# Convolution taps held at their written place on VectorE, and the layer norm's sums taken with the convolutions

## The chip, the cores and the metric

The kernel runs on one core of one Trainium2 chip. That core has five engines with instruction queues of their own: TensorE (PE, matrix multiplication; the loading of its stationary operand is shown apart as PEld), VectorE (DVE), ScalarE (ACT), GpSimd (POOL) and SyncE (SP), which here only issues DMA transfers. They meet through semaphores. The metric is the device time of one execution in microseconds (us); less is better.

## What is computed

One layer of a streaming encoder: 512 rows (time steps) of width 2048, float32. Cut to what matters here, where `h` is the normalised input, and `proj = h @ w_in` is split into its parts:

```python
qkv, z_a, b_raw, a_raw, glu_in, z_b, gate_logits = jnp.split(proj, _split_points(), axis=-1)
...
o_a = gated_delta_chunked(q, k, v, g_log, beta)      # 16 heads; inverts a 64x64 triangle per chunk
o_a = rmsnorm(o_a, g_dn_out[i]).reshape(B, S, DN_WIDTH).astype(x.dtype) * jax.nn.silu(z_a)
y_a = o_a @ w_br_a[i]
u = jax.nn.glu(glu_in, axis=-1)
u = causal_depthwise_conv(u, w_dw[i]) + b_dw[i]      # 31 taps along time, for each channel
u = jax.nn.silu(layernorm(u, ln_g[i], ln_b[i])) * jax.nn.silu(z_b)
y_b = u @ w_br_b[i]
...
mixed = (gate_a * y_a + gate_b * y_b) @ w_out[i]
x = x + rmsnorm(mixed, g_post[i])
e = p[i] @ w_ple_proj[i]
x = x + rmsnorm(jax.nn.sigmoid(x @ w_ple_gate[i]) * e, g_ple[i])
```

The layer norm goes over the 2048 channels of each time step; in the kernel channels lie on partitions, 128 to a tile, so that its sums run over 16 tiles and then over the partitions.

## The kernel before

**Matmuls.** A float32 operand is split into a high and a low part; each product is three matmuls of 128x512 (high·high, high·low, low·high). `gemm_cm` makes one 128x512 output tile from 16 pieces along the depth, so 48 matmuls in one PSUM bank (L181, L183, L185). Its weights come by SP as `raw` tiles of 512 KB. ScalarE casts the high part (L127), VectorE subtracts for the low one (L128), and up to three such pieces are prepared ahead.

**Jobs, ticks and side work.** The tiles of `gemm_cm` are queued as `jobs`. After every matmul `tick()` counts down each generator in `active`; one whose count is used up runs to its next `yield n`, which sets the next count (its own period if no n is given). So all other work is *written* between the matmuls of the gemms at a chosen number of ticks. The framework then works out each engine's order from what was written, and may place an instruction earlier or later among those of its engine; `pin(...)` (`keep_in_program_order`) holds one at its written place. Before the change only the multiplications of the inverse (L900) are pinned.

**Stages, in order.**

1. Load and transpose the input; form the operands of the block products.
2. `z_phase`: z and the gated pair (GLU) by seven block products (P1, Q5, P6, P7, P3, P2, Q4) in six blocks `jp`: before the change the first two are z, the other four the gated pair. A gated block's result is transposed and stored as `u0_dram`, the input of the convolutions.
3. 64 tiles of `gemm_cm`, and one for beta: q, k, v of the 16 heads, with silu(z_b) and gate tiles between. After every six q/k/v tiles a generator `group(g)` for two heads is spawned: transposes; `pg` (L866, the products of keys and queries); W; copies into `Ud` on ScalarE (L882); the transpose UT (L889) on VectorE; the triangular inverse, 31 pairs of multiplication and sum on VectorE (L900, L901); its transposes Vd (L908) and Tc (L916); after 22 ticks `py` on TensorE (L922), the first to read Tc; `pz` (L925) and `pd` (L937); then two scans over the chunks (`head_scan`), whose psA, psB and psS on TensorE alternate with short work on VectorE (`Xz`, S) and ScalarE. There are eight groups.
4. Branch A: `o_a` is split (`split_oa`), 16 tiles multiply it by `w_br_a`. Sums for the later `w_out` products run on GpSimd's DMA queue (`presum`).
5. The layer norm, while left-over gate tiles run; then branch B (`w_br_b`), which needs all 16 normalised tiles and begins with `finish()`, so with all side work done.
6. The output products, the embedding gate, and the output.

**The convolutions** run beside stages 2 to 4, tile by tile of 128 channels. `dwconv(i)` loads a tile `u`, starts `uc` on ScalarE (L307), adds 30 taps on VectorE (L310), loads the next tile at tap 22, adds the result to `acc`, and stores it. One `yield` per tap makes a step. Steps come from `conv_side` in stage 2 (every second call, from block 3 on), then by a pace: `tempo[0]` ticks to a step, 14 in stage 3 and 4.9 in branch A. `group` sets the pace to 0 at its start, grants 11 steps behind the Ud copies (`H_BURST`), and turns the pace on again at Vd. `convs()` ends when all tiles are done.

The layer norm before: reload 16 tiles, mean by one matmul with ones (L1066), subtract it, square, add the squares, variance by four one-column matmuls (L1081), then scale, silu, multiply with z_b and split.

`slots` is a pool of 21 SBUF tiles of 128x512; `s2` and `lop` take over the memory of the heads in stage 4.

Of the kernel before, what the change touches and what calls it, by code (L numbers as in the profile page):

```python
# [15 lines left out]
P = 128  # L16
T = 512
# [65 lines left out]
def _body(ctx, tc, A, out):  # L83
# [203 lines left out]


    u_t = [None] * NK
    done = [0]  # L290
    acc = []
    cpool = [slots, "s"]

    u_in = {}

    def load_u(i):
        u_in[i] = cpool[0].tile([P, T], F32, tag=cpool[1], name="u")
        nc.sync.dma_start(u_in[i], u0_dram[i])

    def dwconv(i):  # L300
        w0 = V_DW + i * TAPS
        if i == 0:
            load_u(0)
            yield
        u = u_in.pop(i)
        y = cpool[0].tile([P, T], F32, tag=cpool[1], name="uc")
        nc.scalar.activation(y, u, AF.Identity, scale=vv(w0 + TAPS - 1), bias=vv(V_BDW + i))  # L307
        yield
        for s in range(1, TAPS):
            nc.vector.scalar_tensor_tensor(y[:, s:], u[:, 0:T - s], vv(w0 + TAPS - 1 - s), y[:, s:], ALU.mult, ALU.add)  # L310
# [11 lines left out]
    tempo = [0, 0]  # L322

    def convs():
        n = 0
        for i in range(NK):
            for _ in dwconv(i):
                n += 1
                yield int(tempo[0] * n) - int(tempo[0] * (n - 1)) if tempo[0] else 3
                while not tempo[0] and not tempo[1]:  # L330
                    yield 2
                if not tempo[0]:
                    tempo[1] -= 1
    conv = convs()


# [17 lines left out]
    def z_phase():  # L354
# [166 lines left out]
        def conv_side():  # L521
            side2[0] += 1
            if side2[0] % 2:
                tempo[:] = [9, 0]
                next(conv)

        for jp in range(6):
            glu = jp >= 2
            conv_on = conv_side if jp >= 3 else None
            more = stepper(gen, 2)  # L530
            ps = run(("P1", "Q5"), (lambda: (more(), conv_side())) if jp >= 4 else more)
            for _ in gen:
# [13 lines left out]
            for t in range(2):  # L546
                tt_(d[t], ps["P3"][t], d[t], ALU.add)
                tt_(s5[t], s5[t], u2[t], ALU.subtract)
                for n, c in ((0, d[t]), (2, s5[t])):
                    if glu:  # L550
                        nc.scalar.activation(c, c, AF.Sigmoid)
                    else:
                        fin(n + t, 2 * jp + 1, c)
            ps = run(("P2", "Q4"), conv_on)
            for t in range(2):
                tt_(s1[t], ps["P2"][t], s1[t], ALU.add)
                tt_(u2[t], ps["Q4"][t], u2[t], ALU.add)
                for n, c, g in ((0, s1[t], d[t]), (2, u2[t], s5[t])):
                    if glu:
                        tt_(c, c, g, ALU.mult)  # L560
                    else:
                        fin(n + t, 2 * jp, c)
            gen = transposed(4 * (jp - 2), (s1, u2)) if glu else iter(())
        finish("form")
# [3 lines left out]
    FILL = 5  # L568
    H_TEMPO, H_BURST = 14, 11
    z_phase()  # L570
    tempo[:] = [H_TEMPO, 0]
    spawn(conv, H_TEMPO, "conv")
    gemm_cm(w_in_tile(BA_TILE), hT, lambda ps: spawn(beta_decay(ps), 5))
# [132 lines left out]

    o_a = [None] * NH

    def conv4(ps, ct):
# [33 lines left out]
    def head_scan(g, hh, G):  # L743
# [62 lines left out]
        for x in range(2):  # L806
            nc.vector.tensor_scalar(oav[:, :, x, :], po[:, :, 1 - x, :], vv(V_GDN), None, ALU.mult)
        o_a[h] = oa

    def group(g):  # L810
        tempo[:] = [0, 0]
        G = dict(ke=[], vh=[])
# [37 lines left out]
        for hh, h, s4, kq, kc, vc in heads:  # L850
# [30 lines left out]
        for r, n, b in ((slice(0, P), P, 0), (slice(32, 64), 32, 32), (slice(96, P), 32, 32)):  # L881
            nc.scalar.copy(Ud[r], U[r, :, b:b + 32].rearrange("p x s -> p s x").unsqueeze(2).broadcast_to([n, 32, 4, 8]))  # L882
        tempo[1] = H_BURST
        yield
        VT = hd.tile([P, 32, 8], F32, tag="VT", name="VT", bufs=1)
# [25 lines left out]
        for qd in (0, 2, 1, 3):  # L911
# [4 lines left out]
            nc.vector.transpose(Tc[r, :, b:b + 32], dst)  # L916
        yield 22
        pz = wps.tile([P, 8, 64], F32, tag="w", name="pz")
# [66 lines left out]
    oT = []  # L985

    def split_oa():
        for h in range(NH):
            oh = low(2 * h, "oh")
            nc.scalar.copy(oh, o_a[h])  # L990
# [47 lines left out]

    jobs.append(lambda: tempo.__setitem__(0, 4.9))
    for _ in range(3):  # L1040
# [5 lines left out]
    for i in range(NK):  # L1046
        gemm_cm(A["w_br_a"][i], oT, evac_ya(i))
        if i + 3 < NK:
            jobs.append(lambda i=i: load_gate(i + 3))
        if i < 7:  # L1050
            rest.popleft()()
# [6 lines left out]
    def layer_norm():  # L1058
        while done[0] < NK:
            yield  # L1060
        for i in range(NK):
            u_t[i] = s2.tile([P, T], F32, tag="s2", name="ur")
            nc.sync.dma_start(u_t[i], u_dram[i])
            yield 3
        pm = lps.tile([P, T], F32, tag="l", name="mean_ps")
        mm(pm, ones, acc[0], start=True, stop=True)  # L1066
        mean = low(0, "mean", F32)
        nc.vector.tensor_scalar(mean, pm, 1.0 / D, None, ALU.mult)
        acc2 = low(0, "acc2", F32)
        for i in range(NK):  # L1070
# [7 lines left out]
        yield  # L1078
        pvr = lps.tile([P, T], F32, tag="l", name="var_ps")
        for tt in range(NTT):  # L1080
            mm(pvr[:, tt:tt + 1], acc2[:, tt * P:(tt + 1) * P], ones[:, 0:1], start=True, stop=True)  # L1081
        yield
        var = lnp.tile([P, NTT], F32, name="var")
        nc.vector.tensor_scalar(var, pvr[:, 0:NTT], 1.0 / D, EPS, ALU.mult, ALU.add)
        rst = lnp.tile([P, NTT], F32, name="rst")
# [13 lines left out]
        for i in range(NK):  # L1099
            u = u_t[i]  # L1100
            nc.vector.tensor_tensor(u, u, rstd, ALU.mult)
            nc.scalar.activation(u, u, AF.Silu, scale=vv(V_LNG + i), bias=vv(V_LNB + i))
# [9 lines left out]
            yield  # L1112

    def load_zb(i):
        zb[i] = low(0, "zb", F32)
        nc.sync.dma_start(zb[i], zb_dram[i])

    jobs.append(lambda: spawn(layer_norm(), 7))
    while rest:
# [485 lines left out]
```

## Time and profile before

| | |
|---|---|
| median of 3 runs | 2524.67 us (2522.82 to 2525.76) |
| profiled execution | 2530.41 us, of which the span from first to last instruction is 2528.6 us |
| TensorE busy | 2469.2 us |
| VectorE busy | 1852.9 us |
| ScalarE busy | 1162.8 us |
| GpSimd busy | 218.0 us |
| mean granted TensorE clock | 0.981 |
| convolution taps (L310) | 480 in all, 342.2 us |
| DMA | 386.51 MB, 153 GB/s |

How to read it: busy time is the union of an engine's instructions. Matmuls are pipelined, so that one of 0.39 us may begin 0.23 us after the one before; a busy TensorE is not one at its peak. The profile gives for each instruction group its line, engine, tiles and shapes, busy time, mean duration in ns, and the idle time of the engine ahead of it with what ended it. The view of waits has us in total, times, and the longest. A row of the windows view has the stretch, its length, and the busy time and number of instructions of each engine (or of one line alone), then the granted clock as a share of the full one, the DMA engines' share and GB/s. A row of the timeline has start, duration, engine, line, operation, output and inputs, and in brackets the idle time before it and what ended that.

### The profile page before, as it was taken

The page shows a single profiled execution, that of the slowest core. Times are in us where ns is not written, and L with a number is a line of the kernel's source. Part 1 is how long each engine was busy: PE and PEld are TensorE (multiplying, and loading weights), DVE is VectorE, ACT ScalarE, POOL GpSimd, SP SyncE. Part 2 cuts the span into 40 slices and gives each one's busy share as a digit, 9 for nine tenths or more (in the row PEclk, how much of TensorE's full clock was granted, in tenths as well). Part 3 has the DMA queues.
Part 4 walks back from the last instruction along what each step waited for, and adds up shares of the span by engine and source line. Part 5 has one row for each costly group of instructions (what it writes and reads, how often), then busy time and mean ns, then how long its engine had stood idle before and what let it go on. Part 6 is the DMA issues. An engine that isn't in the chain of part 4 may idle for free.

```text
span 2528.6 us, 33524 instructions
## 1 busy us (share of the span) xinstructions
PE 2469.2 (98%) x11978; PEld 2013.1 (80%) x11978; DVE 1852.9 (73%) x3539; ACT 1162.8 (46%) x2287; POOL 218.0 (9%) x292
## 2 busy tenths in 40 slices
PE   8999999999999999999999999999999999999998
PEld 7888878878878787878878788888788888788886
DVE  7878779788677777777786869899736655567644
ACT  6545544455635454445546364522225623444532
POOL 0000000011000000000100000232312100000000
PEclk9999999999989898989999899999999999999999
DMA  7576655554322222323222223798957733564642
GB/s 262 168 197 184 183 169 165 176 159 134 115 78 88 72 100 72 100 69 111 78 94 82 94 71 109 221 274 258 297 184 214 263 120 105 201 228 166 206 173 75
DMA packets 147592, 386.51 MB, mean 153 GB/s; under 512 B 16608, under 2 KB 29152, under 8 KB 147424
## 3 DMA queue, kind: packets, MB, share of 16 engines
q1 hardware_dynamic: 125920, 327.73, 38.6%
q0 software_dynamic: 20352, 54.54, 9.6%
q10 hardware_dynamic: 1152, 2.10, 0.3%
q8 instruction: 94, 1.54, 0.2%
q14 instruction: 74, 0.61, 0.1%
HBM read 331.87 MB, written 52.43 MB: 152 GB/s over the span
## 4 chain that ended last, share of the span: by engine, by line
PE 72%; DVE 18%; issue 4%; ACT 3%; DMA 2%; SPq 0%; POOL 0%; DVEq 0%; POOLq 0%; ACTq 0%
PE g L185 12%; PE g L181 12%; PE g L183 12%; DVE uc L310 7%; PE zp L479 5%; PE zp L481 5%; PE zp L480 5%; DVE w L128 3%; DVE prod L900 2%; PE f L1292 2%; PE f L1293 2%; PE f L1291 2%; PE f L1457 2%; PE f L1455 2%; PE f L1456 2%
## 5 line engine op out<-in xcount | busy, mean ns | idle before, releaser
L185 PE MATMUL g<-hh,w 128*128 128x512 f32 x1552 | 624.2, 402 | 5.8 <-DVE w L128 5.8
L183 PE MATMUL g<-hl,w 128*128 128x512 f32 x1552 | 624.4, 402 | 0.0
L181 PE MATMUL g<-hh,w 128*128 128x512 f32 x1552 | 622.4, 401 | 0.0
L127 ACT CAST w<-raw 128x512 fp32r<-128x512 f32 x588 | 358.4, 618 | 514.4 <-PE g L185 383.1
L128 DVE TENSOR_TENSOR w<-raw,w 128x512 fp32r<-128x512 f32 x588 | 405.3, 693 | 227.1 <-ACT w L127 225.2
L185 PEld LDWEIGHTS g<-hh,w 128*128 128x128 f32 x1552 | 296.4, 191 | 65.6 <-DVE w L128 9.8
L310 DVE SCALAR_TENSOR_TENSOR uc<-u,vec,uc 128x503 f32<-128x503 f32 (+22 forms) x480 | 342.2, 732 | 3.1 <-ACT uc L307 0.9
L183 PEld LDWEIGHTS g<-hl,w 128*128 128x128 f32 x1552 | 296.0, 191 | 57.6 <-issue 2.1
L181 PEld LDWEIGHTS g<-hh,w 128*128 128x128 f32 x1552 | 296.2, 191 | 56.5 <-issue 1.1
L714 DVE SCALAR_TENSOR_TENSOR cv<-g,vec,cv 128x511 f32<-128x511 f32 x144 | 107.0, 743 | 26.0 <-ACT cv L712 25.4
L479 PE MATMUL zp<-w,zoh 128*128 128x512 f32 x256 | 101.6, 397 | 0.0
L181 PE MATMUL g<-oh,w 128*128 128x512 f32 x256 | 99.8, 390 | 1.5 <-ACT w L127 1.5
L481 PE MATMUL zp<-w,zol 128*128 128x512 f32 x256 | 100.7, 393 | 0.0
L185 PE MATMUL g<-oh,w 128*128 128x512 f32 x256 | 100.1, 391 | 0.6 <-DVE w L128 0.6
L480 PE MATMUL zp<-w,zoh 128*128 128x512 f32 x256 | 99.8, 390 | 0.8 <-DVE w L361 0.8
L183 PE MATMUL g<-ol,w 128*128 128x512 f32 x256 | 99.6, 389 | 0.0
L181 PE MATMUL g<-uh,w 128*128 128x512 f32 x256 | 99.6, 389 | 0.0
L183 PE MATMUL g<-ul,w 128*128 128x512 f32 x256 | 99.6, 389 | 0.0
L185 PE MATMUL g<-uh,w 128*128 128x512 f32 x256 | 99.6, 389 | 0.0
L466 ACT CAST w<-zt 128x512 fp32r<-128x512 f32 x96 | 59.4, 621 | 71.6 <-PE zp L481 50.1
L900 DVE TENSOR_TENSOR prod<-UT,VT 128x2 f32<-128x2 f32 (+30 forms) x248 | 87.9, 354 | 3.2
L1014 POOL DMA_DIRECT2D wsum<-in_w_out x96 | 75.2, 819 | 137.1 <-DMA g_dram<-gt 46.5
(372 smaller groups left out, 4565.0 us busy)
## 6 DMA issues: line engine op xcount, KB each, us to landing
raw<-in_w_in SPq DMA_DIRECT2D x194, 512.0 KB, 3.3
raw<-in_w_glu SPq DMA_DIRECT2D x48, 512.0 KB, 4.1
wsum<-in_w_out POOLq DMA_DIRECT2D x96, 256.0 KB, 6.4
raw<-in_w_ple_gate SPq DMA_DIRECT2D x40, 512.0 KB, 3.4
zraw<-in_w_glu SPq DMA_DIRECT2D x64, 256.0 KB, 4.7
raw<-in_w_br_a SPq DMA_DIRECT2D x32, 512.0 KB, 6.3
wo_sums<-wsum POOLq DMA_DIRECT2D x64, 256.0 KB, 5.4
raw<-in_w_br_b SPq DMA_DIRECT2D x32, 512.0 KB, 3.3
```

Of the source, the lines that this page charges most:

```text
L127: nc.scalar.copy(hi, rq)
L128: nc.vector.tensor_tensor(lo, rq, hi.bitcast(F32), ALU.subtract)
L181: mm(ps, wh, rh, start=(k == 0), stop=False)
L183: mm(ps, wh, rl, start=False, stop=False)
L185: mm(ps, wl, rh, start=False, stop=(k == NK - 1))
L310: nc.vector.scalar_tensor_tensor(y[:, s:], u[:, 0:T - s], vv(w0 + TAPS - 1 - s), y[:, s:], ALU.mult, ALU.add)
L479: mm(ps[pr][t], lh, wh, start=q + n == 0, stop=False)
L480: mm(ps[pr][t], lh, wl, start=False, stop=False)
L481: mm(ps[pr][t], ll, wh, start=False, stop=q == 3 and n == 1)
L714: nc.vector.scalar_tensor_tensor(y[:, s:], ps[:, 0:T - s], vv(w0 + 3 - s), y[:, s:], ALU.mult, ALU.add)
L900: pin(nc.vector.tensor_tensor(pv_, um, vm, ALU.mult))
L1014: nc.gpsimd.dma_start(t[n], WO[jp, blk, q][:, cs[n]], **(dict(accum_op=ALU.add) if add else {}))
```

## The change

Taps are pinned. The convolution gets its mean per time step of the first tile (`c0`) subtracted from every tile, and sums of the tiles and of their squares are kept as it goes. The layer norm starts from these sums and reloads tiles as it normalises them.

```diff
     def dwconv(i):
...
         for s in range(1, TAPS):
-            nc.vector.scalar_tensor_tensor(y[:, s:], u[:, 0:T - s], vv(w0 + TAPS - 1 - s), y[:, s:], ALU.mult, ALU.add)
+            pin(nc.vector.scalar_tensor_tensor(y[:, s:], u[:, 0:T - s], vv(w0 + TAPS - 1 - s), y[:, s:], ALU.mult, ALU.add))
             if s == 22 and i + 1 < NK:
                 load_u(i + 1)
             yield
         if i == 0:
-            acc.append(slots.tile([P, T], F32, tag="s", name="acc"))
-            nc.gpsimd.tensor_copy(acc[0], y)
+            pc0 = gps.tile([P, T], F32, tag="g", name="c0_ps")
+            mm(pc0, cc(C_ONES), y, start=True, stop=True)
+            sums_d["c"] = ctile("c0")
+            nc.vector.tensor_scalar(sums_d["c"], pc0, 1.0 / P, None, ALU.mult)
+            yield
+        nc.vector.tensor_tensor(y, y, sums_d["c"], ALU.subtract)
+        nc.sync.dma_start(u_dram[i], y)
+        if i == 0:
+            sums_d["1"], sums_d["2"] = ctile("acc"), ctile("acc2")
+            nc.scalar.copy(sums_d["1"], y)
+            nc.scalar.activation(sums_d["2"], y, AF.Square)
         else:
-            nc.vector.tensor_tensor(acc[0], acc[0], y, ALU.add)
-        nc.sync.dma_start(u_dram[i], y)
+            nc.scalar.activation(u, y, AF.Square)
+            nc.vector.tensor_tensor(sums_d["1"], sums_d["1"], y, ALU.add)
+            yield
+            nc.vector.tensor_tensor(sums_d["2"], sums_d["2"], u, ALU.add)
         done[0] += 1
```

`taps(n)` takes n steps; `paced()` takes one at every `tempo[0]` ticks, and none while it is 0:

```diff
+    def taps(n):
+        for _ in range(n):
+            next(conv, None)
+
+    def paced():
+        n = 0
+        while done[0] < NK:
+            if tempo[0]:
+                taps(1)
                 n += 1
-                yield int(tempo[0] * n) - int(tempo[0] * (n - 1)) if tempo[0] else 3
...
+                yield int(tempo[0] * n) - int(tempo[0] * (n - 1))
+            else:
+                yield 2
```

The block products, and the pace:

```diff
-        blocks = [(A["w_z"], 0), (A["w_z"], 1)] + [(A["w_glu"], j) for j in range(4)]
+        blocks = [(A["w_glu"], j) for j in range(4)] + [(A["w_z"], j) for j in range(2)]
...
-            glu = jp >= 2
-            conv_on = conv_side if jp >= 3 else None
+            glu = jp < 4
+            conv_on = conv_side if jp >= 1 else None
...
-    H_TEMPO, H_BURST = 14, 11
+    H_TEMPO, A_TEMPO = 12, 5.7
```

In `group(g)`: two steps ahead of `pg`, six behind the Ud copies, none in the inverse:

```diff
             G["vh"].append(vh)
+        taps(2)
         yield
         pgs = []
...
-        tempo[1] = H_BURST
-        yield
+        for _ in range(3):
+            taps(2)
+            yield 4
         VT = hd.tile([P, 32, 8], F32, tag="VT", name="VT", bufs=1)
...
-        yield 22
+        yield 14
         pz = wps.tile([P, 8, 64], F32, tag="w", name="pz")
```

Twelve of the sixteen `o_a` tiles go to DRAM and come back; the sums move to the pool `s2`:

```diff
+        if h < KEEP_O:
+            nc.sync.dma_start(o_dram[h], oa)
...
+    for k in sums_d:
+        t = ctile("sd")
+        nc.scalar.copy(t, sums_d[k])
+        sums_d[k] = t
...
     def split_oa():
         for h in range(NH):
+            if h + 2 < KEEP_O:
+                load_o(h + 2)
             oh = low(2 * h, "oh")
```

Ten instead of seven of the left-over tiles are placed between those of branch A (`if i < 10`), which leaves eight behind it. The layer norm, spawned with period 9 instead of 7:

```diff
         while done[0] < NK:
             yield
-        for i in range(NK):
-            u_t[i] = s2.tile([P, T], F32, tag="s2", name="ur")
-            nc.sync.dma_start(u_t[i], u_dram[i])
-            yield 3
...
-        mm(pm, ones, acc[0], start=True, stop=True)
+        mm(pm, ones, sums_d["1"], start=True, stop=True)
+        pvr = lps.tile([P, T], F32, tag="l", name="var_ps")
+        for tt in range(NTT):
+            for n, k in enumerate(("1", "2")):
+                mm(pvr[:, n * NTT + tt:n * NTT + tt + 1], sums_d[k][:, tt * P:(tt + 1) * P], ones[:, 0:1], start=True, stop=True)
+        for i in range(3):
+            load_ur(i)
+        yield
...
-        for i in range(NK):
-            u = u_t[i]
-            nc.vector.tensor_tensor(u, u, mean, ALU.subtract)
-            sq = low(0, "lsq", F32) if i else acc2
-            nc.scalar.activation(sq, u, AF.Square)
-            if i:
-                nc.vector.tensor_tensor(acc2, acc2, sq, ALU.add)
-            yield 12
...
         for i in range(NK):
             u = u_t[i]
+            if i + 3 < NK:
+                load_ur(i + 3)
+            nc.vector.tensor_tensor(u, u, mean, ALU.subtract)
             nc.vector.tensor_tensor(u, u, rstd, ALU.mult)
```

The variance is then the mean of the squares less the square of the mean, both taken of the tiles less `c0`.

More of the change, by code (lines that the diff above doesn't have):

```diff
@@ L314, in dwconv @@
         if i == 0:
-            acc.append(slots.tile([P, T], F32, tag="s", name="acc"))
-            nc.gpsimd.tensor_copy(acc[0], y)
-        else:
-            nc.vector.tensor_tensor(acc[0], acc[0], y, ALU.add)
-        nc.sync.dma_start(u_dram[i], y)
+            pc0 = gps.tile([P, T], F32, tag="g", name="c0_ps")
[9 more added lines that the diff above has]
+            nc.scalar.activation(sums_d["2"], y, AF.Square)
+        else:
+            nc.scalar.activation(u, y, AF.Square)
+            nc.vector.tensor_tensor(sums_d["1"], sums_d["1"], y, ALU.add)
+            yield
+            nc.vector.tensor_tensor(sums_d["2"], sums_d["2"], u, ALU.add)
         done[0] += 1
-    tempo = [0, 0]
     def convs():
+        for i in range(NK):
+            yield from dwconv(i)
+    conv = convs()
+    tempo = [0]
+    def taps(n):
+        for _ in range(n):
+            next(conv, None)
+    def paced():
         n = 0
-        for i in range(NK):
-            for _ in dwconv(i):
+        while done[0] < NK:
+            if tempo[0]:
+                taps(1)
                 n += 1
-                yield int(tempo[0] * n) - int(tempo[0] * (n - 1)) if tempo[0] else 3
[L330 to L334, printed above, removed]
+                yield int(tempo[0] * n) - int(tempo[0] * (n - 1))
+            else:
+                yield 2
     LO, HI = slice(0, 256), slice(256, 512)
@@ L523, in conv_side @@
             if side2[0] % 2:
-                tempo[:] = [9, 0]
-                next(conv)
+                taps(1)
         for jp in range(6):
-            glu = jp >= 2
-            conv_on = conv_side if jp >= 3 else None
+            glu = jp < 4
+            conv_on = conv_side if jp >= 1 else None
             more = stepper(gen, 2)
-            ps = run(("P1", "Q5"), (lambda: (more(), conv_side())) if jp >= 4 else more)
+            ps = run(("P1", "Q5"), (lambda: (more(), conv_side())) if jp >= 2 else more)
             for _ in gen:
@@ L985, in _body, with load_o @@
     oT = []
+    def load_o(h):
+        o_a[h] = slots.tile([P, T], F32, tag="s", name="ol")
+        nc.sync.dma_start(o_a[h], o_dram[h])
+    for h in range(2):
+        load_o(h)
     def split_oa():
         for h in range(NH):
+            if h + 2 < KEEP_O:
+                load_o(h + 2)
             oh = low(2 * h, "oh")
@@ L1112, in layer_norm, with load_ur @@
             yield
+    def load_ur(i):
+        u_t[i] = s2.tile([P, T], F32, tag="s2", name="ur")
+        nc.sync.dma_start(u_t[i], u_dram[i])
     def load_zb(i):
```

41 lines of the change are left out of this document (21 added, 20 removed).

## The prediction

> **What bounds the kernel now.** The page is read first: which engine has no time left.
>
> ```profile
> span 2528.6 us, 33524 instructions
> ...
> PE 2469.2 (98%) x11978; PEld 2013.1 (80%) x11978; DVE 1852.9 (73%) x3539; ACT 1162.8 (46%) x2287; POOL 218.0 (9%) x292
> ```
>
> TensorE works 98% of the span. So an edit on another engine is worth only what it takes out of TensorE's idle time, or out of the time that its matmuls need. The longest of TensorE's waits (us in total, times, longest) says where it idles:
>
> ```profile
> PE py L922 <- DVE Tc L916: 26.3, 6, 5.2
> ```
>
> In six of the eight head groups TensorE comes to `py` (L922) and VectorE hasn't yet delivered `Tc`, the end of the triangular inverse. Next, the stretches from one group's `pg` (L866) to the next one's. All seven hold the same TensorE work (635 matmuls).
>
> ```profile
> 668.20:790.20 122.00, 116.44 (x635) 93.34 (x634) 92.50 (x224) 57.76 (x141) 7.79 (x9) 0.93 0.25 85
> 790.20:911.20 121.00, 115.48 (x635) 92.60 (x634) 92.62 (x224) 57.75 (x140) 7.73 (x9) 0.94 0.25 83
> 911.20:1031.80 120.60, 115.94 (x635) 94.27 (x634) 94.57 (x224) 57.98 (x140) 7.22 (x9) 0.93 0.26 86
> 1031.80:1151.80 120.00, 115.28 (x635) 93.61 (x634) 94.61 (x224) 57.87 (x140) 7.23 (x9) 0.94 0.26 86
> 1151.80:1259.10 107.30, 107.30 (x635) 89.00 (x634) 79.47 (x198) 57.51 (x140) 8.46 (x9) 1.00 0.29 94
> 1259.10:1377.70 118.60, 112.35 (x635) 91.06 (x634) 90.95 (x219) 57.55 (x140) 7.46 (x9) 0.96 0.27 87
> 1377.70:1500.10 122.40, 116.86 (x635) 93.61 (x634) 92.66 (x224) 57.72 (x140) 7.73 (x9) 0.93 0.24 81
> ```
>
> The columns are the stretch, its length, busy time of PE, PEld, DVE, ACT and POOL, the granted clock, and DMA. The fifth stretch takes 107.30 us, has no idle TensorE and a full clock; the other six take 118.6 to 122.4 us. The difference is larger than the idle time: TensorE is also *busy* 5 to 9.5 us longer, at a clock of 0.93 to 0.96. What the wait leaves behind shows in the timeline of the third group:
>
> ```profile
> 960.09 0.39 PE L183 MATMUL g<-hl,w 128*128 128x512 f32 x1
> 964.38 0.28 PE L922 MATMUL py<-Tc,W 32*32 32x32 f32 x2 [3.91 <-DVE Tc L916]
> ...
> 969.92 0.63 PE L185 MATMUL g<-hh,w 128*128 128x512 f32 x1
> 970.35 0.63 PE L181 MATMUL g<-hh,w 128*128 128x512 f32 x1
> ```
>
> After 3.91 us of idling the matmuls start 0.43 us apart. How far apart they start otherwise, the fifth stretch's inverse shows below (0.226 us). So a wait of 4 to 5 us is paid about three times: once as idle time, and the rest in a stretch of matmuls at half clock. Last: what separates the groups that wait from those that don't? The convolution taps (L310) inside the eight inverses, from UT (L889) to Tc:
>
> ```profile
> 677.00:734.00 57.00, 22.03 (x30) 0.97 0.33 111
> 799.00:856.00 57.00, 21.93 (x30) 0.98 0.32 107
> 920.00:966.00 46.00, 13.27 (x18) 0.96 0.31 103
> 1040.00:1087.00 47.00, 13.27 (x19) 0.98 0.31 101
> 1160.00:1196.00 36.00, 0.00 (x0) 1.00 0.37 124
> 1269.00:1316.00 47.00, 12.35 (x17) 0.94 0.32 107
> 1386.00:1444.00 58.00, 22.11 (x30) 0.97 0.31 105
> 1508.00:1542.00 34.00, 0.00 (x0) 1.00 0.41 139
> ```
>
> Six inverses hold 17 to 30 taps and last 46 to 58 us; two hold none and last 34 to 36 us; exactly these two have no wait. Written are only 11 taps in each, so taps written later are run early here. The trace of before thus holds the experiment: an inverse without taps isn't waited for.
>
> **The change, part by part.**
>
> *Pinned taps, none written inside the inverse.* Eight steps of the convolutions stand ahead of the inverse (two before `pg`, three pairs behind the Ud copies), the pace is off until Vd (L908), and pinned taps can't slide past the pinned L900. What is late next? The fifth group:
>
> ```profile
> 1154.38 6.14 ACT L882 COPY Ud<-W 128x1024 f32<-128x1024 f32 x3 [2.67 <-DVE W L870]
> 1160.55 1.25 DVE L889 STREAM_TRANSPOSE UT<-Ud 128x1024 f32<-128x1024 f32 x1 [4.85 <-ACT Ud L882]
> ...
> 1194.21 1.38 DVE L916 STREAM_TRANSPOSE Tc<-VP 32x256 f32<-32x256 f32 x3
> 1195.15 0.39 PE L185 MATMUL g<-hh,w 128*128 128x512 f32 x1
> ...
> 1196.96 0.39 PE L183 MATMUL g<-hl,w 128*128 128x512 f32 x1
> 1197.28 0.69 PE L922 MATMUL py<-Tc,W 32*32 32x32 f32 x32
> ```
>
> Tc ends at 1195.59, `py` starts at 1197.28: VectorE has 1.7 us to spare. (From 1195.15 to 1196.96 eight matmuls start, 0.226 us each.) Six taps in the Ud window cost 6 × 0.73 = 4.4 us (22.03/30) and fit into the 4.85 us in which VectorE stands idle for Ud. The pace restarts just ahead of Tc, so one tap may run before it: 0.73 us, leaving about 1.0 us. The written distance from `pg` to `py` is unchanged (8 ticks more before the inverse, 22 → 14 behind it; a tick is one matmul). So I take the six waits as gone and every stretch as the fifth: 831.9 (the seven lengths) − 7 × 107.3 = **−80.8 us**. The eighth group didn't wait and stays.
>
> *A step that starts a convolution behind Ud.* Counting the written steps (66 in the block-product stage, 28 up to the first group, some 23 a group), a new convolution begins right behind the Ud copies in the first and the last group. Its ACT `uc` (L307, 0.81 us below) is then queued behind 6.14 us of Ud, its four pinned taps wait for it, and behind them the inverse: 0.8 + 4 × 0.73 = 3.7 us late against 1.0 us to spare. If ACT runs `uc` earlier it costs nothing; if not, the first group waits 2.7 us, and with a half-clock stretch some 10 us. I take +3 us, the bare wait, and keep 0 and 10. The last group has more room, 3.7 us from Tc's end to `py`:
>
> ```profile
> 1541.42 0.44 DVE L916 STREAM_TRANSPOSE Tc<-VP 32x256 f32<-32x256 f32 x1 [0.26 <-ACT VP L915]
> 1545.58 0.69 PE L922 MATMUL py<-Tc,W 32*32 32x32 f32 x32
> ```
>
> *Added TensorE work*, which nothing hides on a full engine:
>
> ```profile
> L1066 PE MATMUL mean_ps<-acc,cst 128*128 128x512 f32 x2 | 1.0, 592 | 0.0
> L307 ACT ACTIVATE uc<-u,vec 128x512 f32<-128x512 f32 x16 | 13.0, 814 | 31.3 <-DMA u<-u_dram 24.1 <-DVE uc L310 7.2
> ```
>
> c0's sum has mean_ps's shape, 1.0 us; four more var columns (one column each, where mean_ps has 512) I take as no dearer: **+2 us**. VectorE gets 16 subtractions of c0 and one scaling, 17 at no more than a tap's 0.73, 12 us; squares and their sums only move. It is busy 73% and waits for others; nothing of it reaches the end while a stretch has room: 79.47 us in the fifth, plus 17 taps for the missing ones, 92 of 107 us.
>
> *Taps spread over the scans.* Some 15 taps per group now fall between Tc and the next group, 12 ticks apart. Before, 12 ran there in the third group, in less room, and TensorE didn't idle:
>
> ```profile
> 966.30:996.00 29.70, 29.70 (x176) 23.61 (x175) 22.48 (x46) 13.96 (x36) 0.63 (x1) 0.78 0.17 54
> 966.30:996.00 29.70, 8.97 (x12) 0.78 0.17 54
> ```
>
> Part of that ran at half clock, so the comparison is kind; a late `Xz` would cost up to a tap, 0.7 us. I take nothing, at most 5 us over all groups.
>
> *Gated pair first; layer norm.* The block products keep their order of loads and matmuls; only the weights swap. In the part of that stage that has taps TensorE idles 3.1 us:
>
> ```profile
> 350.00:525.00 175.00, 171.88 (x756) 138.76 (x757) 150.81 (x243) 87.54 (x154) 8.69 (x10) 1.00 0.59 173
> ```
>
> I leave that (between −3 and +5: two more slots are held by sums, 66 steps instead of 38 run there). VectorE's scaling of c0 waits once for TensorE, and splits queue behind it; the four pieces ahead (24 matmuls, 5.4 us) cover that. By the written order the last tap comes 1350 ticks into branch A's 1392, and the layer norm needs 37 steps of 9 ticks, 333 of the 384 ticks of eight tiles: 51 ticks or 11.6 us to spare, so branch B starts on time. Twelve `o` tiles go out and come back, 24 transfers of 256 KB on SP; a store waits there for VectorE with weight loads behind it, and a reload is issued two steps (14 ticks, 3.2 us) before ACT reads it, and the three weight pieces prepared ahead (36 matmuls × 0.226 = 8.1 us) cover either, at a landing of 5 us (the u loads' median, quoted below).
>
> *Sum*: −80.8 + 3 + 2 = −75.8. The profiled execution took 2530.41 us (span 2528.6), so 2454.6; the median of the runs is 5.7 us lower, 2524.67: **2449 us**.
>
> [...]
>
> **The rivals.**
>
> *Some waits stay.* The spare time is 1.0 us by one group's row, and the half clock makes a wait of a few us cost 80.8/6 = 13.5 us. One to three left: 2462 to 2490. For it: the convolution start in the first group, and that the taps are only moved. Against: 17 to 30 taps leave where 4 to 5 us were short.
>
> *It doesn't do what it says.* Other work (weight splits, L714) fills the inverse as the taps did, or six taps push UT back, and all six waits remain: 2515 to 2525. Against: the two inverses without taps weren't filled up.
>
> *Slower: a pinned tap that waits blocks VectorE.* Place: the seven convolutions of branch A. A tap now waits at its place for `uc`, that for `u` from DRAM (the L307 row: 24.1 us waited), and the weight splits queue behind it. From load to first tap are 11 steps × 5.7 ticks × 0.226 = 14.2 us, and prepared pieces cover 8.1 more, so it decides once a load needs about 26 us to idle TensorE for 4. Seven such starts at 13.5 us are 94, against −75.8: 2543. Against it:
>
> ```profile
> u<-u_dram SPq DMA_DIRECT2D x16, 256.0 KB, 4.8
> ```
>
> The median landing is 4.8 us. [...]
>
> **How the numbers follow.** Forecast (2440 to 2462) 0.66; some waits stay 0.20; better, down to 2436, with other gaps closed too, 0.04; no effect 0.05; slower 0.05. The range 2438 to 2490 holds the first two and leaves out the ends. About 0.2%, 5 us, is what a measurement can tell: faster 0.92 (the no-effect case half), same 0.03, slower 0.05.
>
> **What would show it.** Right: no L310 between UT and Tc, no `py` wait over 1.5 us, every stretch between `pg`s near 107 us at clock 1.00, VectorE filled between W and UT. Wrong: a `py` wait in the first group (convolution start), an idle TensorE in branch A behind L307 (pinned taps), or before branch B's first matmul (layer norm late). The forecast fails if half-clock stretches remain with no wait ahead of them.

## The result: 0.7% faster, a quarter of what was forecast

| | median | lowest to highest | profiled execution | its span |
|---|---|---|---|---|
| before, run beside it | 2523.74 us | 2521.73 to 2525.76 | 2530.41 us | 2528.6 us |
| changed | 2505.94 us | 2505.17 to 2509.62 | 2505.17 us | 2503.4 us |

The ratio is 0.9932, with a 95% interval of 0.9915 to 0.995. Between the two profiled executions 25.2 us went, where 75.8 were forecast. The medians differ by less, 17.8 us, since the profiled execution of before took longer than any of the four timed ones beside the change; stages are compared in single profiled executions throughout.

The page of the changed kernel, the same lines as shown for before:

```profile
span 2503.4 us, 33557 instructions
...
PE 2455.9 (98%) x11988; PEld 2001.9 (80%) x11988; DVE 1887.5 (75%) x3559; ACT 1171.2 (47%) x2295; POOL 221.4 (9%) x291
```

TensorE is still busy 98%. First the stages: both kernels' windows from one mark to the next (first block product, end of the block products, first group's `pg`, last group's `pg`, start and end of branch A, start of branch B; columns as in the prediction). Before:

```profile
94.30:570.80 476.50, 472.59 (x2065) 382.35 (x2064) 391.99 (x633) 240.09 (x415) 26.46 (x36) 1.00 0.62 175
570.80:668.20 97.40, 97.03 (x448) 78.44 (x446) 74.31 (x140) 56.26 (x108) 16.04 (x14) 1.00 0.39 128
668.20:1500.10 831.90, 799.65 (x4439) 647.48 (x4438) 637.38 (x1531) 404.14 (x980) 53.62 (x63) 0.95 0.26 86
...
1629.40:1883.20 253.80, 251.66 (x1104) 206.62 (x1104) 196.49 (x306) 62.58 (x103) 76.47 (x110) 1.00 0.88 256
1883.20:2005.90 122.70, 122.70 (x542) 100.97 (x542) 78.86 (x130) 74.54 (x113) 25.12 (x35) 1.00 0.80 254
```

The changed kernel:

```profile
94.30:577.90 483.60, 477.66 (x2082) 385.25 (x2082) 401.15 (x652) 241.71 (x419) 24.44 (x35) 1.00 0.61 173
577.90:679.50 101.60, 97.91 (x443) 78.95 (x441) 82.40 (x153) 59.37 (x110) 17.59 (x14) 1.00 0.38 121
679.50:1472.70 793.20, 778.23 (x4428) 630.01 (x4427) 642.50 (x1513) 406.03 (x986) 57.22 (x64) 0.98 0.29 94
...
1601.20:1883.90 282.70, 282.70 (x1249) 234.09 (x1248) 231.89 (x345) 79.19 (x128) 87.83 (x127) 1.00 0.90 259
1883.90:1980.60 96.70, 92.84 (x406) 75.67 (x405) 62.94 (x106) 59.44 (x84) 15.29 (x21) 0.98 0.78 256
```

The seven stretches between the `pg`s, where nearly the whole gain was expected, gave 831.9 − 793.2 = 38.7 us instead of 80.8 − 3. Given back were 483.6 − 476.5 = 7.1 us in the block products, 4.2 us ahead of the first group, and 2.9 us in branch A and the layer norm taken together (282.7 + 96.7 against 253.8 + 122.7; left-over tiles moved from the second window to the first). Part of this is work that lies elsewhere: 16 transposes of the last gated block now fall into the block products' window, and 11 large matmuls (11 × 0.226 = 2.5 us) that ran in the first stretch now run ahead of the first `pg`. The rest is level. Branch A is full: 282.70 us busy of 282.70. Two kernels of the next section whose head stage is the same (`z_quiet`, `ur_early`) take 793.2 and 795.6 us for the seven stretches, so differences of about 2 us between single executions tell nothing.

What remains in the stretches? Two of them, in the windows view:

```profile
793.60:905.00 111.40, 109.72 (x635) 89.15 (x634) 91.80 (x217) 58.30 (x141) 7.98 (x9) 1.00 0.29 95
905.00:1018.10 113.10, 111.39 (x635) 90.14 (x634) 91.41 (x217) 58.18 (x141) 8.09 (x9) 0.98 0.29 96
```

All seven take 111.4 to 114.9 us; none is at 107.3. TensorE's waits name the same operation as before (`py`), with smaller and more numerous waits:

```profile
PE py L948 <- DVE Tc L942: 9.9, 14, 3.1
...
PE pz L951 <- DVE Tc L942: 2.0, 6, 0.4
PE r_ps L711 <- DVE tg L706: 1.8, 1, 1.8
PE r_ps L711 <- DVE E_mk L716: 1.5, 1, 1.5
```

And the taps (now L314) from UT to Tc, in the third inverse (46 us and 18 taps before; six of the eight have five now, two have three):

```profile
914.00:953.00 39.00, 3.61 (x5) 1.00 0.33 116
```

Five taps are still between UT and Tc. Where they come from shows in VectorE's timeline of the third group:

```profile
908.80 1.50 DVE L314 SCALAR_TENSOR_TENSOR uc<-u,vec,uc 128x499 f32<-128x499 f32 x2
913.76 1.25 DVE L915 STREAM_TRANSPOSE UT<-Ud 128x1024 f32<-128x1024 f32 x1 [3.45 <-ACT Ud L907]
915.03 0.69 DVE L128 TENSOR_TENSOR w<-raw,w 128x512 fp32r<-128x512 f32 x1
915.64 0.73 DVE L314 SCALAR_TENSOR_TENSOR uc<-u,vec,uc 128x497 f32<-128x497 f32 x1
...
916.90 0.73 DVE L314 SCALAR_TENSOR_TENSOR uc<-u,vec,uc 128x496 f32<-128x496 f32 x1
917.54 0.15 DVE L926 TENSOR_TENSOR prod<-UT,VT 128x2 f32<-128x2 f32 x1
917.66 0.73 DVE L314 SCALAR_TENSOR_TENSOR uc<-u,vec,uc 128x495 f32<-128x495 f32 x1
...
949.71 0.69 DVE L314 SCALAR_TENSOR_TENSOR uc<-u,vec,uc 128x493 f32<-128x493 f32 x1
950.54 0.43 DVE L942 STREAM_TRANSPOSE Tc<-VP 32x256 f32<-32x256 f32 x1
```

and in ScalarE's:

```profile
907.56 6.16 ACT L907 COPY Ud<-W 128x1024 f32<-128x1024 f32 x3 [2.66 <-DVE W L895]
...
914.38 1.66 ACT L127 CAST w<-raw 128x512 fp32r<-128x512 f32 x3
```

Only two of the six taps ran while VectorE waited for Ud (the row of 908.80; a tap is told by its width, 499 down to 494). The next (497) stands behind a weight split (L128), and that split's cast (L127) on ScalarE stands behind the 6.16 us of Ud copies. UT is not pinned and was placed ahead of split and taps. The last two (495 and 494) ran even behind the inverse's first pinned multiplication (L926 at 917.54), though they are written ahead of it: in the source that multiplication follows UT's memset (L916), which isn't pinned, and it is held behind that, not behind the taps. So VectorE idled 3.45 us where the prediction had six taps, four taps ran inside the inverse, and a fifth (the paced one, 493) right ahead of Tc. TensorE's timeline shows what that costs:

```profile
951.12 0.22 PE L948 MATMUL py<-Tc,W 32*32 32x32 f32 x2 [0.58 <-DVE Tc L942]
951.70 0.69 PE L948 MATMUL py<-Tc,W 32*32 32x32 f32 x30 [0.36 <-DVE Tc L942]
...
953.04 1.21 PE L951 MATMUL pz<-W,Tc 64*64 64x64 f32 x30 [0.35 <-DVE Tc L942]
...
955.19 0.63 PE L183 MATMUL g<-hl,w 128*128 128x512 f32 x1
955.62 0.63 PE L185 MATMUL g<-hh,w 128*128 128x512 f32 x1
```

A wait of 0.58 us, two more behind it as the four transposes of Tc come one by one (1.29 us in all), and then matmuls 0.43 us apart again: small waits can still bring half a clock.

### The profile page after: what moved, and what is told of

It is laid out like the page before. It is cut to its first block, busy times and chain, and to the rows that moved or that the text cites. A ratio compares the mean times of both kernels' runs of the same rounds, so it can differ in the third digit from the quotient of the medians.

```text
span 2503.4 us, 33557 instructions
## 1 busy us (share of the span) xinstructions
PE 2455.9 (98%) x11988; PEld 2001.9 (80%) x11988; DVE 1887.5 (75%) x3559; ACT 1171.2 (47%) x2295; POOL 221.4 (9%) x291
## 4 chain that ended last, share of the span: by engine, by line
PE 75%; DVE 13%; issue 4%; ACT 3%; DMA 3%; POOL 1%; SPq 0%; DVEq 0%; POOLq 0%; ACTq 0%
PE g L185 13%; PE g L183 13%; PE g L181 13%; PE zp L501 5%; PE zp L502 5%; PE zp L500 5%; DVE prod L926 3%; DVE w L128 3%; PE f L1331 2%; PE f L1332 2%; PE f L1330 2%; DVE VT L927 2%; PE f L1496 2%; PE f L1494 2%; PE f L1495 2%
## 5 line engine op out<-in xcount | busy, mean ns | idle before, releaser
L127 ACT CAST w<-raw 128x512 fp32r<-128x512 f32 x588 | 359.7, 618 | 521.5 <-PE g L185 425.6
L128 DVE TENSOR_TENSOR w<-raw,w 128x512 fp32r<-128x512 f32 x588 | 408.0, 697 | 211.5 <-ACT w L127 210.4
L314 DVE SCALAR_TENSOR_TENSOR uc<-u,vec,uc 128x511 f32<-128x511 f32 (+14 forms) x480 | 352.8, 735 | 5.2
L926 DVE TENSOR_TENSOR prod<-UT,VT 128x2 f32<-128x2 f32 (+30 forms) x248 | 87.0, 351 | 5.6
```

The lines of the kernel that those rows point to most:

```text
L127: nc.scalar.copy(hi, rq)
L128: nc.vector.tensor_tensor(lo, rq, hi.bitcast(F32), ALU.subtract)
L314: pin(nc.vector.scalar_tensor_tensor(y[:, s:], u[:, 0:T - s], vv(w0 + TAPS - 1 - s), y[:, s:], ALU.mult, ALU.add))
L926: pin(nc.vector.tensor_tensor(pv_, um, vm, ALU.mult))
```

## Experiments

The theory: the taps that got behind UT cost the missing 42 us in the stretches, through small waits and the half clock behind them. Rivals: taps anywhere on VectorE slow the matmuls' operands (the scans' share); the pins themselves hold VectorE up; the remaining waits come from too short a written distance to `py`. Each kernel below is the changed one with one edit, unless said.

**No taps at all from the first group to the last** (`no_taps`), **the eight ahead of the inverse left out** (`no_burst`), **the paced ones left out** (`no_scan`). Each guards the pinned instruction:

```diff
+            if not quiet[0]:
                 pin(nc.vector.scalar_tensor_tensor(y[:, s:], ...))
```

> The changed kernel with all taps left out from the first head group to the last (they are missing from the convolution). It gives the floor of a stretch. If the taps in the scans cost what no_burst (109.7 us a stretch) has over the fifth stretch before (107.3), the stretches are 107 to 107.5 us; if something else of the change does (the stores of o, the squares and sums), they stay at 109 us or above.

> The changed kernel with the eight taps written around pg and Ud in each group left out (64 taps of the convolution missing); those in the scans stay. Theory A: stretches of 109 to 110 us, no half clock. Theory B: stretches of 112 to 113 us.

> The changed kernel with the taps at the 12-tick pace between Tc and the next group left out; the eight around pg and Ud stay. Theory A: the one tap ahead of Tc goes (0.7 us), so the wait shrinks to about zero and a stretch falls by 2 to 3 us, to 110 to 111. Theory B: stretches of 107 to 109 us, nearly all of the excess over 107.3.

**Four of the eight** (`four`): the two before `pg` and one pair behind the Ud copies; branch A's pace takes up the others.

```diff
-        for _ in range(3):
-            taps(2)
-            yield 4
+        taps(2)
+        yield 12
...
-    H_TEMPO, A_TEMPO = 12, 5.7
+    H_TEMPO, A_TEMPO = 12, 5.1
```

> The changed kernel with four steps per group (two ahead of pg, two behind the Ud copies) instead of eight: the four whose taps came behind UT are taken in branch A instead, at 5.1 ticks a step (5.7 before). Theory A (late Tc by taps behind UT): UT to the end of Tc 36.3 instead of 39.2 us with UT no later, no Tc wait, no half clock, stretches of 110 to 110.5 us, the whole about 2484 us. Theory B (taps in the scans): stretches stay at 112 or more, above 2498 us. If branch A has no room for 32 more taps on VectorE, its 283 us grow.

The seven stretches in one window each, `no_taps`, then `no_burst`, then `four`:

```profile
679.10:1436.70 757.60, 754.00 (x4430) 623.55 (x4429) 543.85 (x1363) 406.15 (x986) 51.25 (x64) 1.00 0.29 98
```

```profile
677.40:1446.20 768.80, 763.51 (x4428) 618.86 (x4427) 609.37 (x1463) 407.73 (x987) 58.27 (x64) 1.00 0.30 97
```

```profile
681.70:1452.50 770.80, 764.83 (x4428) 621.06 (x4427) 624.90 (x1485) 405.66 (x985) 56.80 (x64) 1.00 0.29 96
```

With the same matmuls as the changed kernel's 4428 to within two, this is a ladder. Seven times 107.3 is 751.1. Without taps it is 757.6 (108.2 a stretch, between the two values expected), with a first wait of 1.4 us at `py` left. The paced taps add 11.2. The two taps before `pg` and the pair in the Ud window add 2.0, no more than two executions differ. The other four, which get behind UT, add 793.2 − 770.8 = 22.4, or 3.2 us a stretch. In `four` the wait for Tc is left in the first group alone:

```profile
PE py L947 <- DVE Tc L941: 2.9, 2, 2.5
```

Its six other stretches take 109.2 to 110.1 us, at full clock. It ran in 2487.13 us, 0.9849 [0.9824, 0.9875] of before. `no_taps` took 2471.15 us, `no_burst` 2480.71 and `no_scan` 2492.86 (one execution each; the median of before beside them was 2523 and 2526).

`no_scan` came out against its expectation. Its stretches sum to 779.3 us, 13.9 less than the changed kernel, near the paced taps' 11.2; but its waits at `py` did not shrink, which they should have if paced taps made them:

```profile
PE py L954 <- DVE Tc L948: 14.3, 14, 3.1
```

They grew from 9.9 us because in groups 2, 3 and 6 the end of a convolution (the subtraction of c0 and the two sums, 2.1 us on VectorE, neither pinned nor left out) now falls between UT and Tc; there the first wait is 2.1 us, in groups 4 and 7 without it 0.6 to 0.7. So the paced taps' price is not in these waits. The windows view and the trace's clock split each sum. Idle is the length less TensorE's busy time, half clock is half of the time granted at 0.50, and the rest is TensorE being busy longer at full clock:

| seven stretches, us | over 751.1 | idle | half clock | rest |
|---|---|---|---|---|
| changed | 42.1 | 15.0 | 13.6 | 13.5 |
| `four` | 19.7 | 6.0 | 1.7 | 12.0 |
| `no_burst` | 17.7 | 5.3 | 0.0 | 12.4 |
| `no_taps` | 6.5 | 3.6 | 1.7 | 1.2 |
| `no_scan` | 28.2 | 16.3 | 10.2 | 1.7 |

The four taps' 22.4 are nearly all idle time and half clock (9.0 + 11.9), as the theory has it. The paced taps are the rest: 12 to 13.5 us with them, 1.2 to 1.7 without, so the first rival holds too, for its part. About half of that lies at `po`, the eight transposes that end a group's scans. TensorE's timeline of the second stretch, `no_taps`, then `no_burst`:

```profile
883.23 1.04 PE L826 MATMUL po<-cst,O 128*128 128x128 f32 x8
```

```profile
881.64 0.60 PE L826 MATMUL po<-cst,O 128*128 128x128 f32 x4
882.43 1.11 PE L826 MATMUL po<-cst,O 128*128 128x128 f32 x4 [0.19 <-DVE O L821]
```

With paced taps their input O comes later from VectorE, and the last four transposes start 0.26 us apart instead of 0.11. Such a delay hardly shows as idle time, because one transpose's record, 0.27 us long, reaches to the next one's start. From the first of the eight to the matmul behind them it is 1.66 us instead of 0.79; over the seven stretches 5.6 us. The remainder is spread over the scans' short matmuls (psA, psB, psS) and the next group's transposes.

**All six taps together with a pinned UT right behind them** (`burst_ut`):

```diff
-        for _ in range(3):
-            taps(2)
-            yield 4
+        taps(6)
...
-        nc.vector.transpose(UTf, Ud...)
+        pin(nc.vector.transpose(UTf, Ud...))
...
-        yield
+        yield 16
```

> The changed kernel with all six taps written directly behind the Ud copies and UT written (and pinned) directly behind them. Theory A (the changed kernel still waits for Tc because four of the six taps got behind UT): from UT to the end of Tc 39.2 us falls to about 36.3 (four taps of 0.73), the Tc waits and the half-clock windows behind them go, a stretch from pg to pg falls from 113 to about 110 us, the whole to about 2486 us. Theory B (the stretches are longer because taps spread over the scans keep VectorE from the short work that TensorE waits for; the Tc wait is minor): stretches within 1 us of 113, the whole above 2500 us.

Result 2497.29 us, 0.9883 [0.9864, 0.9901], not the 2486 expected. The taps and UT keep their written order, and in the third group no tap of the six is inside the inverse, yet a price remains. VectorE's timeline of the third group:

```profile
909.81 3.82 DVE L314 SCALAR_TENSOR_TENSOR uc<-u,vec,uc 128x499 f32<-128x499 f32 x5
916.10 0.69 DVE L128 TENSOR_TENSOR w<-raw,w 128x512 fp32r<-128x512 f32 x1 [2.47 <-ACT w L127]
...
917.35 1.24 DVE L913 STREAM_TRANSPOSE UT<-Ud 128x1024 f32<-128x1024 f32 x1
```

Five taps do fit into the Ud window, as the prediction had it. Then a split comes between the fifth and the sixth, which are written with nothing between them: a pin sets what goes ahead, and doesn't keep unpinned work out. The split waits 2.47 us for its cast behind the Ud copies, and UT starts behind the sixth tap at 917.35, though the Ud copies ended at 914.79. The first stretch waits 3.77 us at `py` and takes 116.6; from the second on, the first wait at `py` is 0.03 to 0.62 us, and the stretches take 110.9 to 113.3.

**`py` eight ticks later** (`py_later`), which gives Tc 8 × 0.226 = 1.8 us:

```diff
-        yield 14
+        yield 22
         pz = wps.tile([P, 8, 64], F32, tag="w", name="pz")
```

> The changed kernel with py written 22 instead of 14 ticks behind Tc; no work of VectorE moves. Theory A: 8 ticks are 1.8 us, more than the 0.6 to 1.1 us that Tc is late, so the Tc waits and their half-clock windows go and a stretch falls from 113 to about 110 us; the whole about 2486 us. Theory B: within 5 us of the changed kernel.

Result 2499.22 us, 0.9886 [0.9863, 0.9909], not the 2486 expected. The waits at `py` nearly go (1.30 us is left in the first group), and part turns into other waits. The next group's `pk` waits for this group's last step, now later: 6.9 us in seven waits, which the changed kernel does not have. And in the second stretch `pd` waits 0.98 and 1.40 us for VP, with half clock behind it:

```profile
791.60:908.90 117.30, 113.16 (x637) 91.55 (x636) 90.95 (x217) 58.83 (x142) 8.21 (x9) 0.97 0.28 90
```

The stretches lose 793.2 − 786.3 = 6.9 us in sum, less than `four`'s 22.4; without the second one, which grew by 5.9, the other six lose 12.8.

**The kernel before with only the pins** (`pin_only`):

```diff
-            nc.vector.scalar_tensor_tensor(y[:, s:], ...)
+            pin(nc.vector.scalar_tensor_tensor(y[:, s:], ...))
```

> The kernel before with nothing changed but the pins on the taps. Written are 11 taps inside each inverse. If the number of taps between UT and Tc sets the wait, it is 8 to 11 taps instead of 17 to 30, the inverse lasts 41 to 43 us, the wait is 2 to 4 us in all groups but the last with half clock behind it, and the whole lies between the two kernels, 2505 to 2520 us. If any tap inside costs a full wait, it is no faster than before.

Result 2501.95 us, 0.9909 [0.9886, 0.9932]; the whole change has 0.9932 [0.9915, 0.995]. It is faster than the 2505 to 2520 expected, and the intervals overlap: as far as these runs tell, the pins alone give as much as the whole change. The stretches, and its largest wait:

```profile
673.70:1475.20 801.50, 778.64 (x4437) 632.06 (x4436) 635.66 (x1520) 401.02 (x980) 60.37 (x64) 0.98 0.27 90
```

```profile
PE py L922 <- DVE Tc L916: 15.9, 12, 3.8
```

With only its written 9 to 11 taps in the inverse, Tc is 1.8 to 3.8 us late instead of 3.9 to 5.2. Moving the taps ahead adds 801.5 − 793.2 = 8.3 us to the gain, of which 2.0 are nine matmuls that left the window (4437 against 4428); the block products, 477.4 us here and 483.6 in the changed kernel, take about the rest.

**No taps in the block products** (`z_quiet`, the same guard there), and **z first, as before, with a step at every call** (`z_order`):

```diff
-        blocks = [(A["w_glu"], j) for j in range(4)] + [(A["w_z"], j) for j in range(2)]
+        blocks = [(A["w_z"], j) for j in range(2)] + [(A["w_glu"], j) for j in range(4)]
...
-            conv_on = conv_side if jp >= 1 else None
+            conv_on = conv_side if jp >= 3 else None
```

> The changed kernel without the taps in the block products (missing from the first convolutions). If these pinned taps make the block products 7 us longer than before (483.6 against 476.5 us), the stage falls to about 477; if it is the fourth block of transposes and stores that now lies inside it, it stays at 482 to 484.

> The changed kernel with the block products back in the order z first, gated pair after, and the convolution's steps there in blocks 3 to 5, one at every call (76 instead of 66). If the order (a fourth block of transposes and stores inside the stage) makes the block products 7 us longer than before, the stage falls from 483.6 to 476 to 479 us and the whole by about 5, to 2501 us. If the slots that the sums hold do, it stays at 482 us or above.

`z_quiet` took 2507.81 us (one execution). Its block products take 483.6 us, as in the changed kernel, with 33 us less on VectorE (368.06 instead of 401.15): the taps there cost nothing. That window and the next in `z_order`:

```profile
95.00:573.30 478.30, 474.27 (x2066) 382.44 (x2065) 405.96 (x659) 241.71 (x419) 23.88 (x35) 1.00 0.61 176
573.30:678.50 105.20, 101.70 (x470) 82.33 (x468) 84.91 (x158) 61.15 (x113) 18.04 (x14) 1.00 0.37 121
```

With z first the stage is 478.3, as expected, with 16 matmuls fewer; the last gated block's transposes fall into the next window again, 105.2 us instead of 101.6. The two windows together take 583.5 us against 585.2, and hold nine large matmuls (2.0 us) that the changed kernel runs behind the first `pg`: the order is worth some 4 us. The whole kernel: 2502.20 us, 0.9918 [0.9902, 0.9935], within the interval of the change.

**Reloads of the layer norm five tiles ahead instead of three** (`ur_early`):

```diff
-        for i in range(3):
+        for i in range(5):
             load_ur(i)
...
-            if i + 3 < NK:
-                load_ur(i + 3)
+            if i + 5 < NK:
+                load_ur(i + 5)
```

> The changed kernel with the layer norm's tiles reloaded five ahead instead of three. If VectorE stands in its queue for a late reload with a weight split behind it (the 3.46 us gap of TensorE at 1940.66 and the half-clock window after it), the stretch from the end of branch A to branch B falls from 96.7 to about 92 us, the whole by about 5. If the reloads are late because SP issues them late anyway, nothing changes.

It was made for this place of the changed kernel, VectorE's timeline, then TensorE's:

```profile
1940.89 1.37 DVE L1135 TENSOR_TENSOR ur<-ur,mean 128x512 f32<-128x512 f32 x2 [2.51 <-DMA ur<-u_dram]
...
1943.38 1.29 DVE L128 TENSOR_TENSOR w<-raw,w 128x512 fp32r<-128x512 f32 x2
```

```profile
1944.12 0.80 PE L185 MATMUL g<-hh,w 128*128 128x512 f32 x1 [3.46 <-DVE w L128]
```

VectorE waits 2.51 us for a reload, the weight splits stand behind it though their casts on ScalarE had ended at 1940.11, and TensorE idles 3.46 us and goes on at half clock, 3.41 us of it. Five ahead, the window to branch B takes 94.7 instead of 96.7 us (about 92 expected); waits of 2.1 and 1.1 us stay. In the whole, 2501.12 us, 0.9918 [0.9903, 0.9932], its interval overlaps the change's, so the whole time leaves it unclear.

**Together** (`best`): `four`, `z_order`, `ur_early`, A_TEMPO 5.2, and the pace started again behind the Tc loop instead of ahead of it. **And `py` six ticks later** (`best_py`, 14 → 20).

> Together: four steps a group instead of eight, the pace turned on again behind Tc instead of ahead of it, the old order of the block products, reloads five ahead, 5.2 ticks a step in branch A. From the run with four steps (2487 us): -6 for the block products, -5 for the layer norm, -3 for the first group, whose convolution start no longer falls behind Ud: about 2473 us, with no Tc wait and no half clock between the first pg and branch B.

> As the one before, with py 20 instead of 14 ticks behind Tc. If no group waits for Tc any more, nothing is left to gain: within 3 us of it. If small waits remain, it is faster by them.

`best` took 2480.76 us (2479.19 to 2482.35), 0.9835 [0.982, 0.985]: short of the 2473 expected, but the fastest of those that compute everything, and faster than both kernels. Its stretches:

```profile
679.20:1452.40 773.20, 764.35 (x4421) 619.79 (x4420) 623.63 (x1483) 404.83 (x980) 55.19 (x64) 1.00 0.29 95
```

That is no better than `four` alone (770.8): the tap ahead of Tc is gone, but `po` now waits (3.9 us in seven waits, 1.1 in `four`), and the first group still waits 2.7 us for Tc. `best_py`, expected within 3 us or faster, is slower, 2488.25 us, 0.9869 [0.9854, 0.9883]: its `po` waits 5.7 us in seven waits, and psB 3.3 us in two, for VP. A later `py` makes the steps behind it in the group late for the next consumer.

## Why the prediction was right in kind and wrong in size

- **"The six waits as gone and every stretch as the fifth", −80.8: this step failed**, by 42.1 us. The long waits are gone and the mechanism held: taps out of the inverse shorten it (third group: 46 to 39 us) and TensorE's half clock mostly goes (PEclk 0.95 to 0.98 over the stretches). But the fifth stretch had no tap in its inverse and six in all, where each stretch of the changed kernel has 22 to 24; the prediction moved the taps and took their new place as free. By the ladder the 42.1 us are 22.4 (four taps behind UT), 11.2 (paced taps), 2.0 (the first four), and 6.5 that stay even without taps (9.0 with the 2.5 us of matmuls that left the first stretch).
- **"Six taps in the Ud window fit into the 4.85 us".** By VectorE's time they do (`burst_ut`: five in 3.82 us). What was missed is what stands between them: splits that need ScalarE, which is busy with Ud for those 6 us. The pin holds a tap behind the split; the unpinned UT goes first. "Pinned taps can't slide past the pinned L900" was wrong as well: two of the six ran behind the first of those multiplications (L926 now).
- **"One tap before Tc, about 1.0 us to spare".** The tap is there (949.71), as forecast. With four more in the inverse it left nothing to spare.
- **A short wait's price.** The prediction counted a long wait at 13.5 us and one of under a microsecond at nothing. Waits of 0.6 to 1.1 us, which it would have called right (its sign was "no `py` wait over 1.5 us"), were not free: with the two small ones behind them they brought 3.4 to 6.8 us at half clock in five of six stretches.
- **First group, +3.** It waits 3.13 us and runs 114.1 us. The step that got among its Ud copies on ScalarE is not the new convolution's start but the end of the one before, its square (L331, 0.63 us). It is the smaller part: UT starts 12.2 us behind `pg` there and 8.8 in the other groups, since pinned taps also stand between VectorE's steps for W, and a cast (L127) that waits for TensorE stands ahead of Ud on ScalarE. Waits of 1.4 to 2.7 us stay there in `no_taps`, `four` and `best`.
- **Taps in the scans, "nothing, at most 5".** Measured 11.2, and not as waits for `Xz`: about half is the late O at `po`. The prediction's row (12 taps, no idle TensorE) was read as free, but this price is hardly idle time.
- **Block products, −3 to +5.** Measured +7.1, not from the taps; some of it is the 16 transposes, which left the next window, 2.0 us are more idle time (5.9 against 3.9), and one stretch of 3.41 us at half clock is new. The 4.2 us more in that window were not forecast: it has 2.5 us of large matmuls more, the transposes less, and 1.8 + 1.5 = 3.3 us of `r_ps` waits, which before did not have. VectorE makes their operands among pinned taps, and `pin_only`, in the old order, waits 3.2 us there too: it comes with the pins.
- **Layer norm.** The prediction counted ticks ("branch B starts on time") and put no wait for the layer norm's own reloads into the sum: their landing has a median of 6.3 us, and TensorE idled 3.46 us. The net of the two windows is +2.9. What it said of the `o` tiles, that the prepared pieces cover their transfers, held: branch A has no idle time.
- **Added TensorE work, +2**, is too small to be told apart in the whole time; c0's sum took the 1.0 us forecast.
- **The rivals.** What came is *some waits stay*, with a milder wait in each of the first seven groups instead of one to three full ones; its best and worst, 2462 and 2490, were both still too low, since it priced whole waits alone. *No effect* is refuted. *Slower* (a pinned tap blocking VectorE in branch A) did not happen: TensorE has no idle time there. ScalarE's wait of `uc` for `u` even fell, from 24.1 to 7.6 us:

```profile
L311 ACT ACTIVATE uc<-u,vec 128x512 f32<-128x512 f32 x16 | 13.0, 814 | 10.4 <-DMA u<-u_dram 7.6 <-DVE sd L334 2.7
```

## What to carry to other kernels

A pin here only fixed an instruction behind the one written before it on its engine: if that one waits for a busy engine, the pinned work waits too, while unpinned work may be placed ahead of it or in between. So look at what stands between the moved work and the place that was to be filled, and on which engine *its* input is made. And a stretch that runs well without some work proves that the work costs there, not that it is free elsewhere: price the new place by the length of a stretch that holds such work against one that doesn't. That TensorE isn't idle there is not enough.

## What the runs showed of the hardware

Half clock does not need a long wait. Behind waits of 1.29 us in sum in the third stretch, the granted clock was half for 3.41 us (second row; the first is the 3.41 us just ahead):

```profile
950.57:953.98 3.41, 2.15 (x64) 1.84 (x64) 2.50 (x6) 3.31 (x6) 0.09 (x1) 1.00 0.03 7
953.98:957.39 3.41, 3.41 (x14) 2.62 (x11) 1.87 (x3) 1.61 (x4) 0.00 (x0) 0.50 0.44 154
```

In the second stretch the same three waits (0.58, 0.36, 0.35 us) left the clock at 1.00, and that stretch is 1.7 us shorter (111.40 against 113.10), half of 3.41. The trace's clock shows one difference: all stretches at half clock in the changed kernel start whole multiples of 3.413 us apart (953.98, 1066.62, 1295.32 and 1407.95 us are 0, 33, 100 and 133 of them on). Laid on that grid, the waits of the third stretch fall into one step of it, in which TensorE was busy 2.15 of 3.41 us, with 32x32 and 64x64 matmuls alone. Those of the second fall into two (837.93 to 844.75), busy 2.39 and 3.13 us, each with some large matmuls. That this decides on the clock isn't shown, nor where a limit between them would lie. In before, each of the six waits at `py` (3.91 to 5.20 us) came with a stretch at a clock of 0.50, of 10.24 us (from 1310.67) to 17.07 us (from 730.40), three to five times 3.41.
